# One subtraction of 2048 columns in place of two of 1024, for the low part of a feed-forward's weight block

## The chip, the cores and the metric

The kernel runs on one core of a Trainium2 chip. The metric is device time in microseconds for one execution. The engines are named as the profile names them: PE is TensorE (matmuls; PEld its weight loads), DVE is VectorE, ACT is ScalarE, POOL is GpSimd, SP is SyncE, which issues the transfers.

## The reference

A trunk of two layers on 256 rows of 1024 channels in float32. A layer is half a feed-forward, a mixer, half a feed-forward, each on a normed input and added to the residual; the mixer of layer 0 is a convolution module, that of layer 1 latent attention. The feed-forwards hold most of the work:

```python
D_MODEL = 1024; SEQ = 256; DEPTH = 2; D_FF = 2816
def swiglu_ffn(h, w1, w3, w2):
    return (jax.nn.silu(h @ w1) * (h @ w3)) @ w2

for i in range(DEPTH):
    h = h + 0.5 * swiglu_ffn(rmsnorm(h, ffn_norm1[i]), ffn1_w1[i], ffn1_w3[i], ffn1_w2[i])
    m = rmsnorm(h, mix_norm[i])
    h = h + (conv_module(m, ...) if i % 2 == 0 else mla(m, ...))
    h = h + 0.5 * swiglu_ffn(rmsnorm(h, ffn_norm2[i]), ffn2_w1[i], ffn2_w3[i], ffn2_w2[i])
return rmsnorm(h, final_norm)
```

## The kernel before

**Two parts of every number.** A float32 product is made of three matmuls with fp32r operands (`mm3`, L333 to L337): high by low, high by high, low by high. So each weight block, 128 partitions by 2048 columns, is loaded into a `raw` tile (4 buffers), copied by ACT to `hi` (a rounded copy, a CAST), and DVE subtracts: `lo = raw - hi`. `hi` and `lo` have 5 buffers each. Both are made in two pieces of 1024 columns (`PIECES = 2`), and PE may start on the first piece when its high and low are there. The first matmul that uses a piece takes its low.

**Blocks.** The list `blocks` names all weight blocks in the order of their use. A feed-forward has 39: for the up projection, chunks of 512 hidden columns with four blocks each; for the down projection, blocks of two rows of tiles. An ordinary block is used by 24 matmuls of 512 columns; `load` brings it and splits it (L247, L248).

**Seven products.** One up chunk and the first four blocks of the down projection of each feed-forward are multiplied as a 2x2 block product with seven products in place of eight (`seven`, `load_seven`, `seven_products`). The seven operands are blocks or sums of blocks: DVE makes a sum of 2048 columns in place in a raw tile (`sub` of whole tiles, L201), then the operand is split as any block (L215, L201). The last operand, number 6, is such a sum. Each product is 12 matmuls, so a block lasts PE half as long as an ordinary one. Between products ACT copies a PSUM bank and DVE adds one to another (L259): the add after product 2 and the one after product 4. Two `order` calls tie the first lows of operands 5 and 6 to these adds.

**Around a chunk.** When a chunk's two sums stand in PSUM (`u`), ACT takes the Silu of one (L970) and DVE multiplies (L972, or L259 where the multiplication is marked urgent); that reads the banks, which then serve the next sums (`o` of the down projection among them: PSUM tag A has four). The product `s` is turned (L485, then transfers through DRAM) and split into Gh and Gl (L862): a gate pair.

**Order.** A scheduler places the instructions of each engine from the program's dependencies and its own timeline; `order(a, b)` adds that a comes after b, `behind` puts a cast behind the last urgent instructions of its engine, and `urgent` gives a group priority. Engines run their queues in order.

Of the kernel before, what the change touches and what calls it, by code (L numbers as in the profile page):

```python
# [11 lines left out]
F32 = mybir.dt.float32  # L12
# [7 lines left out]
P = 128  # L20
D = 1024
S = 256
NT = S // P
# [3 lines left out]
HB = 2048  # L27
# [62 lines left out]
def trunk(ctx: ExitStack, tc: tile.TileContext, x, xt, first, pos, invf, gfin, wdw,  # L90
          f1w13, f1w2, f2w13, f2w2, cw1, cw2, wa, wuq, wukv, wo, wpair, out):
    nc = tc.nc
# [12 lines left out]
    def uid(s):  # L105
        n_uid[0] += 1
        return f"{s}_{n_uid[0]}"
# [12 lines left out]
        return [("seven", j, four, group) for j in range(7)]  # L120

    blocks = []
    conv_block = {}
    for i in range(2):
        for w13, w2 in ((f1w13, f1w2), (f2w13, f2w2)):

            n_ffn = 2 * i + (w13 is f2w13)
            for cc_ in range(5):
                if cc_ in SEVEN_UP.get(n_ffn, ()):
                    four = [w13[i, m, 2 * cc_ + a_] for a_ in range(2) for m in range(2)]  # L130
                    blocks += seven(four)
                    continue
                for m in range(2):
                    blocks += [w13[i, m, 2 * cc_ + a_] for a_ in range(2)]
            blocks += [w13[i, a_, 10] for a_ in range(2)]
            if n_ffn in SEVEN_DOWN:
                blocks += seven([w2[i, a_] for a_ in range(4)])
            blocks += [w2[i, a_] for a_ in range(4 if n_ffn in SEVEN_DOWN else 0, NF // 2)]
            if w13 is f1w13:
                if i == 0:  # L140

                    for m in (-1, -2, -3, -4, *CONV_TILES):
                        blocks += [cw2[-m - 1] if m < 0 else ("whole", cw1[m])]
                        conv_block[m] = len(blocks) - 1
                else:
                    blocks += [wa[0], wa[1], wa[2][:, :1280], wa[3][:, :1280]]
                    blocks += [wuq[2], wuq[0], wukv[0], wukv[1], wuq[1]]
                    blocks += [wo[a_] for a_ in range(H // 2)]
    loaded = []
# [8 lines left out]
    def behind(ins):  # L158

        for first in ahead_of.get(ins.ins.engine, [])[-BEHIND:]:  # L160
            order(ins, first)


    casts = {}
# [5 lines left out]
    placed = []  # L170
# [19 lines left out]
    def load_seven(j, four, b, pieces):  # L190
        hi = wp.tile([P, HB], F32R, tag="hi", name=uid("hi"))
        lo = wp.tile([P, HB], F32R, tag="lo", name=uid("lo"))
        n = len(loaded)
        if j == 0:
            b[11], b[12] = fetched(four[0]), fetched(four[1])
        elif j == 1:
            b[22] = fetched(four[3])
        elif j == 2:
            b[21] = fetched(four[2])
        def sub(out, left, right):  # L200
            ins = nc.vector.tensor_sub(out, left, right)  # L201
            behind(ins)
            return ins

        if j == 1:
            sub(b[11], b[12], b[11])
            sub(b[12], b[22], b[12])
        elif j == 2:
            thirds[n] = sub(b[11], b[22], b[11])
        elif j == 6:  # L210
            sub(b[11], b[21], b[11])
        raw = b[(11, 11, 11, 21, 12, 22, 11)[j]]
        for i in range(pieces):
            c = slice(i * HB // pieces, (i + 1) * HB // pieces)
            casts[n, i] = nc.scalar.copy(hi[:, c], raw[:, c]), sub(lo[:, c], raw[:, c], hi[:, c].bitcast(F32))  # L215
            behind(casts[n, i][0])
        return hi, lo

    def load(src, pieces=1):
        if isinstance(src, tuple) and src[0] == "seven":  # L220
            return load_seven(*src[1:], pieces)
        if isinstance(src, tuple):
            raw = rawp.tile([P, HB], F32, tag="raw", name=uid("raw"))
            nc.sync.dma_start(raw, src[1])
            return raw
        n = src.shape[-1]
        there = len(loaded) in raws
        raw = raws.pop(len(loaded))[0] if there else rawp.tile([P, HB], F32, tag="raw", name=uid("raw"))
        hi = wp.tile([P, HB], F32R, tag="hi", name=uid("hi"))
        lo = wp.tile([P, HB], F32R, tag="lo", name=uid("lo"))  # L230
        if there:
            pass
        elif len(loaded) < 7:

            for i in range(pieces if len(loaded) < 4 else 1):
                c = slice(i * n // pieces, (i + 1) * n // pieces) if len(loaded) < 4 else slice(n)
                fetch(raw[:, c], src[:, c])
        else:
            dma = nc.sync.dma_start(raw[:, :n], src)
            if turns:  # L240

                order(dma, turns[-1].ins)
        for i in range(pieces):
            c = slice(i * n // pieces, (i + 1) * n // pieces)

            low = nc.gpsimd if len(loaded) == conv_block[-4] else nc.vector
            casts[len(loaded), i] = (nc.scalar.copy(hi[:, c], raw[:, c]),  # L247
                                     low.tensor_sub(lo[:, c], raw[:, c], hi[:, c].bitcast(F32)))  # L248
            for cast in casts[len(loaded), i] if len(loaded) not in placed else ():
                behind(cast)  # L250
        return hi, lo

# [49 lines left out]
    for k in range(KT):  # L302
        c = slice(k % 4 * 512, k % 4 * 512 + 512)
# [176 lines left out]
    def turn_blocks(pool, src, n, tag, after=(), b=None):  # L480


        w = n * P
        t = pool.tile([P, 512], F32, tag=tag + "t", name=uid(tag + "t"), bufs=2)
        last_turn[0] = nc.vector.transpose(t[:, :w], src.rearrange("p (t j q) -> p j t q", t=n, q=32))  # L485
        d = dram.tile([P, w], F32, tag=tag + "d", name=uid(tag + "d"), bufs=4)
        dv = d.rearrange("(j p) (i c) -> i p j c", p=32, c=32 * n)
        for i in range(4):
            dma = nc.sync.dma_start(dv[i], t[32 * i:32 * i + 32, :w].rearrange("p (j c) -> p j c", j=4))
            for a in after:  # L490
                order(dma, a.ins)
        if b is None:
            b = pool.tile([P, 512], F32, tag=tag + "b", name=uid(tag + "b"), bufs=2)
        last_read[0] = nc.sync.dma_start(b[:, :w], d)
        return b[:, :w].rearrange("p (i t q) -> p t i q", i=4, q=32)

# [346 lines left out]
    gates = []  # L843
# [7 lines left out]
    def ffn_in(act, X, make_next, beside, apart, seven_up, seven_down):  # L851
# [48 lines left out]
        for c in range(6):  # L900
# [18 lines left out]
            for m in range(0 if u else 1 if both else 2):  # L919
                parts = weights(KT // kn, c > 0 or m > 0)  # L920
# [17 lines left out]
                for i, (k, tb, *kinds) in enumerate(steps):  # L938
                    hi, lo = parts[k // kn]
# [35 lines left out]
        if seven_down:  # L975
            both = (xp.tile([P, KT, S], F32R, tag=tag, name=uid("rows")) for tag in ("Xh", "Xl"))
            late = {2: None, 3: None}
            o.seven({**first_form, **forms_of(down_sums[1:], *both, late)}, late)
            for gate in gates[-2 * NT:]:
                for ins, cast in zip(gate, casts[n_used[0] + 1, 0]):  # L980
                    order(ins, cast.ins)
        stage.append("down")
# [456 lines left out]
    def mla_in(act, X, make_next, cc, sn):  # L1439
# [61 lines left out]
        parts = weights(3, False)  # L1501
# [4 lines left out]
        last = None  # L1506
        for tb in range(NT):
# [5 lines left out]
            last = last_low[0]  # L1513
# [37 lines left out]
        for tb in range(NT):  # L1551
            u = bank("A", "qr")
            qu.append(u)
            for k in range(4):
                after = (last,) if k == 0 else turned if (tb, k) == (0, 2) else ()
                last = mm3(u, CQh[:, k, tbs(tb)], CQl[:, k, tbs(tb)], hi[:, k * 512:(k + 1) * 512],
                           lo[:, k * 512:(k + 1) * 512], k == 0, k == 3, after)
# [14 lines left out]
        last = nope(part, QN, 4, CQh, CQl, 512, 0, (0, 4), turned)  # L1572
        for t in range(NT):
            b = transposed(kd[t], 0, 1, (last,))
# [5 lines left out]
        for tb in range(NT):  # L1580
            b = transposed(qr[tb], 0, 4, (last,), turns_of[tb]).rearrange("p (j t) -> p j t", t=P)
            for parity in range(2):
                half, rest = (slice(64 * i, 64 * i + 64) for i in (parity, 1 - parity))
                high = QR[half, parity, :, tbs(tb)]
# [8 lines left out]
        for tb in range(NT):  # L1593
            for d in range(2):
                b = bank("A", "v")
                for k in range(2):
                    c = slice(k * D + d * 512, k * D + d * 512 + 512)
# [7 lines left out]
        score_last, maxima, powers, scaled, copies, late = [], [], [], [], [], []  # L1605

        def scores(hd):
            b = bank("B", "sc")
            sc = {0: b[:, :P], 1: b[:, P:P + S]}
            last = None  # L1610
            for qb in range(NT):
                n = (qb + 1) * P
                three = [(QN[:, hd, tbs(qb)], KN[:, hd, :n]), (QA[hd % 2, qb][:, hd // 2], KA[:, :n]),
                         (QR[:, hd % 2, hd // 2, tbs(qb)], KR[:, hd % 2, :n])]
                for i, (rows_of, keys) in enumerate(three if qb == 0 else three[1:] + three[:1]):
                    mm = nc.tensor.matmul(sc[qb], rows_of, keys, start=i == 0, stop=i == 2)  # L1616
                    if last is not None:
                        order(mm, last.ins)
                    last = mm
            score_last.append(last)  # L1620
            return softmax(sc)
# [52 lines left out]
        for j, i, lows in ((0, 0, maxima[2]), (0, 1, scaled[0]), (1, 0, scaled[1]), (1, 1, scaled[2])):  # L1674
            high, low = casts[n_used[0] + j, i]
# [187 lines left out]
```

## Time and profile before

| | us |
|---|---|
| median of 3 runs | 892.11 |
| lowest, highest | 892.09, 892.71 |
| profiled execution | 891.44 |
| its span in the profile | 889.5 |
| PE busy | 882.0 |
| DVE busy | 770.4 |
| ACT busy | 580.2 |

The span is the time from the first to the last instruction of the profiled execution; the rest of its time lies around it. A row of a timeline gives start and duration in us from the span's start, engine, line, operation, output and input; "x2" is two instructions in a row, and brackets give the idle time before and what ended it.

### The profile page before, as it was taken

What the parts mean: (1) busy time and instruction counts of PE and PEld (TensorE: products, weight loads), DVE (VectorE), ACT (ScalarE), POOL (GpSimd) and SP (SyncE); (2) the same over time, 40 slices, a digit from 0 to 9 for tenths busy, and PEclk for the clock granted to TensorE, in tenths of its full rate; (3) what the DMA queues carried; (4) which work ended last, traced back from release to release, by engine and by line L of the source; (5) the groups of instructions that cost most, each with busy time, mean ns of one, the idle gap of its engine ahead of it and who ended that gap; (6) DMA issues with size and microseconds to landing.
All of it is one profiled execution on the core that took longest, in us unless ns stands there. A gap on an engine that the chain in (4) does not pass through costs nothing.

```text
span 889.5 us, 12294 instructions
## 1 busy us (share of the span) xinstructions
PE 882.0 (99%) x4209; PEld 741.9 (83%) x4209; DVE 770.4 (87%) x1114; ACT 580.2 (65%) x1005; POOL 104.8 (12%) x227
## 2 busy tenths in 40 slices
PE   9999999999999999999999999999999999999997
PEld 7888887898988888888888888888899888888886
DVE  6899999789999998999498989995778689989973
ACT  7667868789887655657275465673676666474752
POOL 1000000079952000000010000001400010000000
PEclk9999999999999999999999999999999999999999
DMA  9884929834216855939759378495643549287541
GB/s 338 297 308 161 398 80 374 300 132 153 96 60 225 307 213 194 365 93 393 251 179 344 97 249 318 142 386 183 221 147 142 190 155 368 80 300 276 192 190 48
DMA packets 71054, 198.94 MB, mean 224 GB/s; under 512 B 12368, under 2 KB 41936, under 8 KB 51664
## 3 DMA queue, kind: packets, MB, share of 16 engines
q1 hardware_dynamic: 70560, 197.47, 61.9%
q8 instruction: 33, 0.54, 0.2%
q10 hardware_dynamic: 432, 0.69, 0.2%
q14 instruction: 29, 0.24, 0.1%
HBM read 181.87 MB, written 16.25 MB: 223 GB/s over the span
## 4 chain that ended last, share of the span: by engine, by line
PE 98%; DVE 1%; issue 0%; ACT 0%; ACTq 0%; DVEq 0%
PE u L333 17%; PE u L337 17%; PE u L336 17%; PE o L333 9%; PE o L337 9%; PE o L336 9%; PE u L1019 3%; PE gate L1019 3%; PE o L1255 3%; PE u L418 2%; PE sc L1616 1%; PE tp L453 1%; PE pairs L1062 1%; DVE lo L201 1%; PE a L337 1%; PE a L336 1%
## 5 line engine op out<-in xcount | busy, mean ns | idle before, releaser
L248 DVE TENSOR_TENSOR lo<-raw,hi 128x1024 fp32r<-128x1024 f32 (+1 forms) x228 | 266.8, 1210 | 29.2 <-ACT hi L247 28.5
L247 ACT CAST hi<-raw 128x1024 fp32r<-128x1024 f32 (+1 forms) x230 | 228.5, 1044 | 72.1 <-DMA raw<-in_f2w 24.3
L337 PE MATMUL u<-hi,Xl 128*128 128x512 f32 x592 | 230.4, 389 | 0.0
L336 PE MATMUL u<-hi,Xh 128*128 128x512 f32 x592 | 230.3, 389 | 0.0
L333 PE MATMUL u<-lo,Xh 128*128 128x512 f32 x592 | 230.2, 389 | 0.0
L215 ACT CAST hi<-raw 128x1024 fp32r<-128x1024 f32 x112 | 111.7, 1049 | 56.7 <-DVE raw L201 46.4
L201 DVE TENSOR_TENSOR lo<-raw,hi 128x1024 fp32r<-128x1024 f32 x112 | 132.0, 1215 | 6.6 <-ACT hi L215 6.5
L337 PEld LDWEIGHTS u<-hi,Xl 128*128 128x128 f32 x592 | 111.1, 188 | 23.6 <-DVE Xl L472 0.5
L336 PEld LDWEIGHTS u<-hi,Xh 128*128 128x128 f32 x592 | 111.1, 188 | 23.1
L333 PEld LDWEIGHTS u<-lo,Xh 128*128 128x128 f32 x592 | 111.1, 188 | 22.9
L333 PE MATMUL o<-lo,Gh 128*128 128x512 f32 (+1 forms) x276 | 106.7, 386 | 0.0
L336 PE MATMUL o<-hi,Gh 128*128 128x512 f32 (+1 forms) x276 | 106.5, 386 | 0.0
L337 PE MATMUL o<-hi,Gl 128*128 128x512 f32 (+1 forms) x276 | 106.5, 386 | 0.0
L444 POOL TENSOR_TENSOR ms<-ss 128x1 f32<-128x1 f32 x16 | 8.1, 509 | 592.8 <-ACT junk L436 592.8
L201 DVE TENSOR_TENSOR raw<-raw,raw 128x2048 f32<-128x2048 f32 x32 | 73.1, 2285 | 0.8 <-DMA raw<-in_f1w 0.2
L333 PEld LDWEIGHTS o<-lo,Gh 128*128 128x128 f32 x276 | 51.8, 188 | 10.6 <-DVE lo L201 0.2
L337 PEld LDWEIGHTS o<-hi,Gl 128*128 128x128 f32 x276 | 51.8, 188 | 10.5
L336 PEld LDWEIGHTS o<-hi,Gh 128*128 128x128 f32 x276 | 51.8, 188 | 10.4
L1108 DVE SCALAR_TENSOR_TENSOR acc<-V,dw,acc 128x128 f32<-128x128 f32 (+1 forms) x174 | 53.9, 390 | 0.0
L970 ACT ACTIVATE s<-u,R 128x512 f32<-128x512 f32 (+1 forms) x48 | 30.9, 647 | 29.5 <-PE u L337 28.7
L1129 ACT ACTIVATE prod<-V,dw 128x128 f32<-128x128 f32 (+1 forms) x128 | 45.6, 415 | 1.9 <-POOL Y L1130 1.0
L806 DVE SCALAR_TENSOR_TENSOR h<-o,rh,h 128x512 f32<-128x512 f32 (+1 forms) x18 | 12.9, 719 | 29.0 <-PE o L337 29.0
(269 smaller groups left out, 1306.6 us busy)
## 6 DMA issues: line engine op xcount, KB each, us to landing
raw<-in_f2w SPq DMA_DIRECT2D x66, 1024.0 KB, 5.6
raw<-in_f1w SPq DMA_DIRECT2D x62, 1024.0 KB, 6.9
raw<-in_cw SPq DMA_DIRECT2D x12, 1024.0 KB, 5.2
gd<-gt SPq DMA_DIRECT2D x160, 64.0 KB, 2.9
gb<-gd SPq DMA_DIRECT2D x24, 256.0 KB, 2.8
rows<-gd SPq DMA_DIRECT2D x16, 256.0 KB, 3.3
raw<-in_wo SPq DMA_DIRECT2D x4, 1024.0 KB, 4.7
hd<-rows SPq DMA_DIRECT2D x56, 64.0 KB, 2.3
```

What stands on the lines that cost most here:

```text
L201: ins = nc.vector.tensor_sub(out, left, right)
L215: casts[n, i] = nc.scalar.copy(hi[:, c], raw[:, c]), sub(lo[:, c], raw[:, c], hi[:, c].bitcast(F32))
L247: casts[len(loaded), i] = (nc.scalar.copy(hi[:, c], raw[:, c]), low.tensor_sub(lo[:, c], raw[:, c], hi[:, c].bitcast(F32)))
L248: low.tensor_sub(lo[:, c], raw[:, c], hi[:, c].bitcast(F32)))
L333: mm = nc.tensor.matmul(o, ah, bl, start=start, stop=False, skip_group_check=seeded)
L336: nc.tensor.matmul(o, ah, bh, start=False, stop=False, skip_group_check=seeded)
L337: return nc.tensor.matmul(o, al, bh, start=False, stop=stop, skip_group_check=seeded)
L970: nc.scalar.activation(s[:, :w], u[0, tb][:, :w], AF.Silu, scale=X.r[tb])
L1019: mm = nc.tensor.matmul(u[:, t], w[:, c], X.x[:, k, t], start=(k == 0), stop=(k == KT - 1))
L1108: dve_last.append(nc.vector.scalar_tensor_tensor(out if j == j1 - 1 else y, v, w, y, op0=ALU.mult, op1=ALU.add))
L1129: prods_last.append(nc.scalar.activation(p, v, AF.Copy, scale=w))
L1255: p = nc.tensor.matmul(o[tb, d], (Zl if kind == "x" else Zh)[:, f, tbs(tb)], (lo if kind == "l" else hi)[:, c], start=(f, kind) == (0, "l" ...
```

## The change

In each feed-forward all blocks but the first four and the last four are entered in `at_once`: 31 of 39, 124 in all. For these the two high casts stay two instructions of 1024 columns, and the low is one subtraction of 2048 columns, which needs both highs. The low then counts as the low of both pieces. Three more edits come with it: `gb` tiles in a feed-forward have three buffers, one more gate pair is ordered behind a cast of the down projection, and the scores of heads 1 and 2 are ordered behind those of the head before.

```diff
+    at_once = set()
...
+            n_first = len(blocks)
...
+            at_once.update(range(n_first + 4, len(blocks) - 4))
...
+        split(n, raw, hi, lo, HB, pieces, nc.vector)
         for i in range(pieces):
-            c = slice(i * HB // pieces, (i + 1) * HB // pieces)
-            casts[n, i] = nc.scalar.copy(hi[:, c], raw[:, c]), sub(lo[:, c], raw[:, c], hi[:, c].bitcast(F32))
-            behind(casts[n, i][0])
+            for cast in casts[n, i] if i == 0 or n not in at_once else casts[n, i][:1]:
+                behind(cast)
         return hi, lo
+
+    def split(n, raw, hi, lo, width, pieces, low):
+        parts = [slice(i * width // pieces, (i + 1) * width // pieces) for i in range(pieces)]
+        if n in at_once:
+            highs = [nc.scalar.copy(hi[:, c], raw[:, c]) for c in parts]
+            whole = low.tensor_sub(lo[:, :width], raw[:, :width], hi[:, :width].bitcast(F32))
+            for i, high in enumerate(highs):
+                casts[n, i] = high, whole
+            return
+        for i, c in enumerate(parts):
+            casts[n, i] = (nc.scalar.copy(hi[:, c], raw[:, c]),
+                           low.tensor_sub(lo[:, c], raw[:, c], hi[:, c].bitcast(F32)))
...
-            b = pool.tile([P, 512], F32, tag=tag + "b", name=uid(tag + "b"), bufs=2)
+            b = pool.tile([P, 512], F32, tag=tag + "b", name=uid(tag + "b"), bufs=3 if tag == "g" else 2)
...
-            for gate in gates[-2 * NT:]:
+            for gate in gates[-2 * NT - 1:]:
                 for ins, cast in zip(gate, casts[n_used[0] + 1, 0]):
                     order(ins, cast.ins)
...
-            last = None
+            last = score_last[-1] if 0 < hd < 3 else None
```

The scheduler places the instructions anew. In the rows below, names carry their tile numbers, which differ between the two programs, and the lines of the program after are its own: the split is L226 (high) and L227 (low), sums of blocks L205, adds L271, Silu L982, multiplication L984.

DVE at the end of the up group of seven in the second feed-forward, before: the lows of operands 3, 4 and 5, the add after product 2, the sum for operand 6, the add after product 4, the low of operand 6.

```order
L201 TENSOR_TENSOR lo_3481<-raw_3304,hi_3480 128x1024 x2
L201 TENSOR_TENSOR lo_3501<-raw_3362,hi_3500 128x1024
L259 TENSOR_TENSOR u_3460<-u_3458,p_561_3498 128x512
L201 TENSOR_TENSOR lo_3501<-raw_3362,hi_3500 128x1024
L201 TENSOR_TENSOR raw_3302<-raw_3372,raw_3302 128x2048
L259 TENSOR_TENSOR u_3459<-u_3458,p_561_3498 128x512
L201 TENSOR_TENSOR lo_3520<-raw_3302,hi_3519 128x1024 x2
```

The same place after:

```order
L227 TENSOR_TENSOR lo_3438<-raw_3265,hi_3437 128x2048
L271 TENSOR_TENSOR u_3418<-u_3416,p_561_3454 128x512
L227 TENSOR_TENSOR lo_3457<-raw_3322,hi_3456 128x2048
L205 TENSOR_TENSOR raw_3263<-raw_3331,raw_3263 128x2048
L271 TENSOR_TENSOR u_3417<-u_3416,p_561_3454 128x512
L227 TENSOR_TENSOR lo_3475<-raw_3263,hi_3474 128x2048
```

The first half of operand 5's low stood ahead of the add; the whole low now stands behind it, and the sum for operand 6 behind both.

ACT at the start of the down projection of the same feed-forward, before: high casts, the Silu of the last chunk's two parts (256 columns), more high casts.

```order
L215 CAST hi_3797<-raw_3703 128x1024 x2
L862 CAST Gh_2920<-gb_3623 128x4x128
L970 ACTIVATE s_3866<-u_3816,R_2859 128x256
L215 CAST hi_3807<-raw_3703 128x1024 x2
L215 CAST hi_3906<-raw_3809 128x1024 x2
L366 CAST rows_3898<-rows_139 128x512
L970 ACTIVATE s_3880<-u_3817,R_3006 128x256
```

The same place after:

```order
L226 CAST hi_3744<-raw_3651 128x1024 x2
L226 CAST hi_3753<-raw_3651 128x1024 x2
L226 CAST hi_3851<-raw_3755 128x1024 x2
L982 ACTIVATE s_3811<-u_3761,R_2828 128x256
L378 CAST rows_3843<-rows_139 128x512
L982 ACTIVATE s_3825<-u_3762,R_2975 128x256
```

The first Silu moved behind four high casts, and the gate's high cast (Gh) to a later place.

DVE there, before: a sum of blocks, the multiplication of the last chunk's first part, its turn, two lows.

```order
L862 TENSOR_TENSOR Gl_2921<-gb_3623,Gh_2920 128x4x128
L485 STREAM_TRANSPOSE gt_3778<-s_3775 128x512
L201 TENSOR_TENSOR raw_3703<-raw_3799,raw_3703 128x2048
L972 TENSOR_TENSOR s_3866<-s_3866,u_3816 128x256
L485 STREAM_TRANSPOSE gt_3869<-s_3866 128x256
L201 TENSOR_TENSOR lo_3808<-raw_3703,hi_3807 128x1024 x2
L201 TENSOR_TENSOR lo_3907<-raw_3809,hi_3906 128x1024 x2
```

The same place after:

```order
L497 STREAM_TRANSPOSE gt_3725<-s_3722 128x512
L205 TENSOR_TENSOR raw_3651<-raw_3746,raw_3651 128x2048
L227 TENSOR_TENSOR lo_3754<-raw_3651,hi_3753 128x2048
L227 TENSOR_TENSOR lo_3852<-raw_3755,hi_3851 128x2048
L984 TENSOR_TENSOR s_3811<-s_3811,u_3761 128x256
```

The multiplication moved behind two lows, the turn of its result with it, and the gate's low out of this place.

More of the change, by code (lines that the diff above doesn't have):

```diff
@@ L242, in load @@
                 order(dma, turns[-1].ins)
[L243 to L249, printed above, removed]
+        split(len(loaded), raw, hi, lo, n, pieces, nc.gpsimd if len(loaded) == conv_block[-4] else nc.vector)
+        for i in range(pieces if len(loaded) not in placed else 0):
+            for cast in casts[len(loaded), i] if i == 0 or len(loaded) not in at_once else casts[len(loaded), i][:1]:
                 behind(cast)
```

## The prediction

> **What bounds the kernel now.** First the page: the span and the shares of the engines.
>
> ```profile
> span 889.5 us, 12294 instructions
> PE 882.0 (99%) x4209; PEld 741.9 (83%) x4209; DVE 770.4 (87%) x1114; ACT 580.2 (65%) x1005; POOL 104.8 (12%) x227
> ```
>
> TensorE (PE) is busy for all but 7.5 us. VectorE (DVE), where the change takes work away, is at 87%, and its time counts only where PE waits for it. The waits of PE, named by line, and the chain that ended last show that such places are few now:
>
> ```profile
> PE o L333 <- DVE lo L201: 0.4, 1, 0.4
> ...
> 1.04 3.99 PE warm L325 x21
> 5.03 22.22 PE u L418 x96
> ...
> 136.75 0.47 PE o L333
> ```
>
> So a faster DVE can give back about half a microsecond, and any new PE wait is added to the span in full: nothing gives PE time back. The question is when each low part is ready, against when PE wants it. The groups by form give the sizes:
>
> ```profile
> L248 DVE TENSOR_TENSOR lo<-raw,hi 128x1024 fp32r<-128x1024 f32 x224 | 263.8, 1217 | 29.2 <-ACT hi L247 28.5
> L201 DVE TENSOR_TENSOR lo<-raw,hi 128x1024 fp32r<-128x1024 f32 x112 | 132.0, 1215 | 6.6 <-ACT hi L215 6.5
> L201 DVE TENSOR_TENSOR raw<-raw,raw 128x2048 f32<-128x2048 f32 x32 | 73.1, 2285 | 0.8 <-DMA raw<-in_f1w 0.2
> ```
>
> A half costs 1.22 us, and a whole I take from the third row: 2.29 us (same operation and width, f32 written instead of fp32r).
>
> **The tight place: the end of a group of seven products.** In the timeline of the second feed-forward's up group, DVE, then ScalarE (ACT), then PE:
>
> ```profile
> 345.57 1.22 DVE L201 TENSOR_TENSOR lo<-raw,hi 128x1024 fp32r<-128x1024 f32 x1 [1.25 <-ACT hi L215]
> 346.71 0.69 DVE L259 TENSOR_TENSOR u<-u,p 128x512 f32<-128x512 f32 x1
> 347.31 1.22 DVE L201 TENSOR_TENSOR lo<-raw,hi 128x1024 fp32r<-128x1024 f32 x1
> 348.44 2.29 DVE L201 TENSOR_TENSOR raw<-raw,raw 128x2048 f32<-128x2048 f32 x1
> 351.21 0.70 DVE L259 TENSOR_TENSOR u<-u,p 128x512 f32<-128x512 f32 x1 [0.49 <-PE u L337]
> 351.84 2.36 DVE L201 TENSOR_TENSOR lo<-raw,hi 128x1024 fp32r<-128x1024 f32 x2
> ...
> 350.76 2.01 ACT L215 CAST hi<-raw 128x1024 fp32r<-128x1024 f32 x2 [1.58 <-DVE raw L201]
> ...
> 345.57 0.39 PE L333 MATMUL u<-lo,Xh 128*128 128x512 f32 x1
> 351.01 0.39 PE L333 MATMUL u<-lo,Gh 128*128 128x512 f32 x1
> 353.73 0.39 PE L333 MATMUL u<-lo,Xh 128*128 128x512 f32 x1
> ```
>
> Products are counted from 0. PE begins product 3 at 345.57, 5 at 351.01, 6 at 353.73: 2.72 us each. The last block is a sum that DVE makes (348.44), whose highs ACT then makes (350.76), and of whose low DVE makes the first half at 351.84, as soon as the first high is there (0.03 us after 350.76 + 1.05). That half ends at 353.06 and PE starts on it at 353.73. A stalled start in the first down group shows what lies between a half's end and PE:
>
> ```profile
> 133.18 2.28 DVE L201 TENSOR_TENSOR raw<-raw,raw 128x2048 f32<-128x2048 f32 x1
> 135.38 2.35 DVE L201 TENSOR_TENSOR lo<-raw,hi 128x1024 fp32r<-128x1024 f32 x2
> ...
> 136.75 0.47 PE L333 MATMUL o<-lo,rows 128*128 128x512 f32 x1 [0.40 <-DVE lo L201]
> 137.05 0.40 PE L336 MATMUL o<-hi,rows 128*128 128x512 f32 x1
> ```
>
> The first half ends at 136.60; the next matmul comes at 137.05 where 0.23 after 136.82 would be full pace: 0.2 us. So the margin in the up group is 353.73 - 353.06 - 0.2 = 0.47 us.
>
> **The change, part by part.**
>
> *DVE time.* 124 pairs become wholes. A pair takes 2.35 (row 135.38), a whole 2.29: 0.06 each, 7.4 us in all. None of it is on PE's path, except at 136.75. [...]
>
> *Term A: the last product of a group.* In the changed order the add that follows product 2 stands ahead of the low of block 5, so the chain begins when PE ends product 2, wherever DVE stands: add 0.20 us after product 3's first matmul (351.21 against 351.01); add to next 0.60 (346.71 to 347.31); whole low to next 2.20 (a 2048 row, 133.18 to 135.38); sum to first high 2.32 (348.44 to 350.76); both highs 2.01; 0.03; whole low 2.29; to PE 0.2. That is 9.85 us, and PE has three products, 8.16. PE waits 1.7 us. The two causes: 1.0 us for the second high, 1.1 us for the second half. What DVE saved earlier cannot help, because the chain starts from PE's own end. It holds for seven of the eight groups (four up, three down): 11.9 us, bounds 10.5 and 12.6 (1.5 and 1.8 each: nothing between low and PE, or 0.3).
>
> *Term A', the first down group.* There the sum stands ahead of block 5's low, and PE waits already (136.75). A whole ends 1.07 us later than the half, bound from below 1.1; the add in front waits for more work than before, up to 1.3 more. I take 1.7.
>
> After each group DVE has a multiplication (0.60) and a whole (2.20) for 2.72 us of PE: 0.08 more, five times, 0.4 us.
>
> *Term B: the first whole of the program.*
>
> ```profile
> 24.44 2.00 ACT L247 CAST hi<-raw 128x1024 fp32r<-128x1024 f32 x2 [0.36 <-DMA raw<-in_f1w]
> ...
> 25.52 1.23 DVE L248 TENSOR_TENSOR lo<-raw,hi 128x1024 fp32r<-128x1024 f32 x1 [5.09 <-ACT hi L247]
> ...
> 27.09 0.39 PE L333 MATMUL u<-lo,Xh 128*128 128x512 f32 x1
> ```
>
> Highs end at 26.44; + 0.03 + 2.29 + 0.2 = 28.96 against 27.09: 1.9 us. A multiplication (0.60) stands ahead of it now, under the highs; bounds 1.5 (the block lands earlier by the 0.36 that ACT waited for it) and 2.2 (half of the 0.60 comes late).
>
> *Term C: a PSUM bank given back later.* In the second to fourth feed-forwards' down groups, product 1 writes a bank that a 256-column multiplication (L972) must have read. In the changed order four high casts stand ahead of its Silu on ACT, and two whole lows ahead of it on DVE; the casts wait for a DVE sum.
>
> ```profile
> 384.54 2.25 DVE L201 TENSOR_TENSOR raw<-raw,raw 128x2048 f32<-128x2048 f32 x1
> 387.08 0.42 DVE L972 TENSOR_TENSOR s<-s,u 128x256 f32<-128x256 f32 x1 [0.29 <-ACT s L970]
> ...
> 388.02 4.63 DVE L201 TENSOR_TENSOR lo<-raw,hi 128x1024 fp32r<-128x1024 f32 x4
> ...
> 391.81 0.39 PE L333 MATMUL o<-lo,s1h 128*128 128x512 f32 x1
> ...
> 559.36 2.25 DVE L201 TENSOR_TENSOR raw<-raw,raw 128x2048 f32<-128x2048 f32 x1
> ...
> 565.89 0.39 PE L333 MATMUL o<-lo,s1h 128*128 128x512 f32 x1
> ...
> 821.26 2.25 DVE L201 TENSOR_TENSOR raw<-raw,raw 128x2048 f32<-128x2048 f32 x1
> ...
> 828.79 0.39 PE L333 MATMUL o<-lo,s1h 128*128 128x512 f32 x1
> ```
>
> Before, the multiplication ends at 387.50, 4 us ahead of PE. After: the sum ends at 386.79, less 0.60 (a 512-column operation, as 346.71 to 347.31) because a gate's low (L862) moved behind it; + 0.03 + 2.01 highs + 0.03 + 2 x 2.20 + 0.42 + 0.2 = 393.28 against 391.81: 1.5 us. The same from 561.61: 2.2, and from 823.51: 1.2. Together 4.9; bounds 0, where DVE comes earlier by 2 us, and 6.7, where the 0.60 isn't saved.
>
> *Cheap edits.* The third buffer of gb costs space and hides the later gate lows. The extra gate pair that is held back is the 0.60 above. The order of three heads' score matmuls moves work of one size inside PE's queue, without a wait that the order shows: 0, bounds -0.3 and 0.3. A raw buffer is freed when its second half has been read, as before, so the weight loads do not move by more than the low does. Behind a waiting low stand multiplications, transposes and with them SP's turn DMAs; where they reach PE is terms A and C.
>
> **Sum.** 11.9 + 1.7 + 0.4 + 1.9 + 4.9 = 20.8 us. The profiled execution took 891.44 us (span 889.5 and 1.9 around it), which becomes 912.2; the median of the runs is 0.67 us above the profiled one: 913.
>
> **Rivals.**
> - *Forecast*: 913, its own range 908 to 918: 0.72.
> - *The banks are free in time*: term C falls away, 908. For it: the wholes take 0.06 us less each, and DVE idles 36 us before its lows (29.2 + 6.6 in the groups). Against: eight wholes stand between two groups, 0.5 us, and three times 1.2 to 2.2 is wanted. 0.10.
> - *TensorE's clock drops after each wait.* At the start 21 matmuls of 256 columns took 3.99 us (0.19 each) where later 96 of 512 took 22.22 (0.23): 0.74 ns a column against 0.45. If each of 12 waits over 1 us brought 3 us at that pace, 3 x (1 - 0.45/0.74) = 1.2 us each, 14 us: 927. Against: the wait at 136.75 was followed by full pace. [...] 0.08.
> - *Not slower.* The mechanism: the chain does not start from PE's end but from DVE's queue, and DVE, 0.06 us earlier per block, has the last block's sum made before PE ends product 2. It decides at the first add: if the sum of term A ends 2.2 us (1.7 and the 0.47 margin) earlier than I place it, PE waits nowhere, and the waits at 136.75 go too: 891.4 - 0.4, 891 to 892 as measured. Against: the order puts the sum behind the add and the whole low. 0.06.
> - *More than one of these together, or a wait I did not see*: 0.04.
>
> **The numbers.** A measurement of this kernel can tell 0.2% (1.8 us) from no change. The range 905 to 920 holds the forecast and the free banks: the lower bounds of A, A' and B without C are 10.5 + 1.1 + 1.5 = 13.1 (891.44 + 13.1 + 0.67 = 905), the upper ones with C and 0.08 after all eight groups 12.6 + 2.4 + 2.2 + 6.7 + 0.6 = 24.5 (917), and 3 us are for a wait I did not see; it leaves out the clock and the case without loss. Slower 0.94; same 0.04 and faster 0.02 out of "not slower".
>
> **What would show it.** In the profile after: PE waits for DVE lo (the split's line) about ten times, 1.7 us each at the last product of a group, the highs' second half ending 0.03 us before the whole low begins; three waits of 1 to 2 us for the multiplication L972 at the first s1h product; DVE busy about 18 us less by single durations (124 x (2 x 1.217 - 2.29)); PE's clock unchanged. Wrong would be: waits of PE under 0.5 us, a whole low that starts before its second high, or the sum ahead of the add in the up groups.

## The result

The kernel after took 915.55 us (median of six runs, 913.75 to 918.41) against 892.24 us before (891.94 to 893.05): a ratio of 1.0262, 95% interval 1.0246 to 1.0278. The change makes the kernel 23.3 us slower, where 20.8 were forecast, and the time lies in the forecast's range of 905 to 920. The profiled execution took 915.71 us. First the head of its page and, from the view of waits, what PE waited for (us in total, times, the longest):

```profile
span 913.9 us, 12149 instructions
PE 886.9 (97%) x4209; PEld 740.8 (81%) x4209; DVE 761.8 (83%) x990; ACT 579.2 (63%) x1005; POOL 105.8 (12%) x227
...
PE u L345 <- DVE lo L227: 8.0, 5, 2.1
PE o L345 <- DVE lo L227: 6.0, 4, 1.5
PE o L345 <- DVE s L984: 4.6, 3, 2.1
...
PE o L345 <- DVE o L271: 0.7, 1, 0.7
PE u L430 <- ACT Xh L659: 0.5, 2, 0.4
PE u L345 <- ACT Xh L617: 0.2, 1, 0.2
```

DVE is busy for less time and PE waits. Lines after the split are 12 further down than before: L227 is the low of a whole, L233 that of a half, L205 a sum of blocks, L271 the add of two banks, L984 the last multiplication of a gate. Nine waits are for a whole low (term B, the seven groups of term A, and one of A'), three for L984 (term C), and one for L271 (the other part of A'). The mean granted clock was 0.999.

The end of the second feed-forward's up group after, the place the prediction worked through, DVE, then ACT, then PE:

```profile
352.81 0.70 DVE L271 TENSOR_TENSOR u<-u,p 128x512 f32<-128x512 f32 x1 [0.65 <-PE u L349]
353.42 2.28 DVE L227 TENSOR_TENSOR lo<-raw,hi 128x2048 fp32r<-128x2048 f32 x1
355.62 2.28 DVE L205 TENSOR_TENSOR raw<-raw,raw 128x2048 f32<-128x2048 f32 x1
...
359.97 2.29 DVE L227 TENSOR_TENSOR lo<-raw,hi 128x2048 fp32r<-128x2048 f32 x1 [1.09 <-ACT hi L226]
...
357.94 2.00 ACT L226 CAST hi<-raw 128x1024 fp32r<-128x1024 f32 x2 [1.78 <-DVE raw L205]
...
357.99 0.39 PE L345 MATMUL u<-lo,Gh 128*128 128x512 f32 x1
362.32 0.50 PE L345 MATMUL u<-lo,Xh 128*128 128x512 f32 x1 [1.46 <-DVE lo L227]
```

The add begins as PE ends product 2 (0.65 us of waiting on PE). Behind it stand the whole low of operand 5 and the sum. The highs follow at 357.94, the whole low at 359.97, 0.03 us after the second high, and PE begins product 6 at 362.32, 4.33 us after product 5, where before it was 2.72: 1.6 us late. The step from the matmul that waited to the next one is 0.34 us in place of 0.23, so 0.11 more is lost at each place of terms A, B and C. At the two places of A' that step was as long before the change, and nothing is added.

The start of that feed-forward's down projection, in the same order of engines:

```profile
392.80 2.25 DVE L205 TENSOR_TENSOR raw<-raw,raw 128x2048 f32<-128x2048 f32 x1
397.19 4.49 DVE L227 TENSOR_TENSOR lo<-raw,hi 128x2048 fp32r<-128x2048 f32 x2 [2.14 <-ACT hi L226]
401.60 0.41 DVE L984 TENSOR_TENSOR s<-s,u 128x256 f32<-128x256 f32 x1
...
398.96 0.46 ACT L982 ACTIVATE s<-u,R 128x256 f32<-128x256 f32 x1
...
402.07 0.50 PE L345 MATMUL o<-lo,s1h 128*128 128x512 f32 x1 [1.30 <-DVE s L984]
```

The Silu ran at 398.96, long before DVE came to its multiplication (401.60); that stood behind two wholes (4.41 us), and these behind the highs of a sum.

One thing in the order listings above needs a correction in words. The half of operand 5's low that stood ahead of the add before the change was its second half: it waits for ACT there (1.25 us at 345.57 in the prediction's rows), and the half behind the add waits for nothing. The line `order(casts[n0 + 5, 0][1], add.ins)` binds the low that `casts` keeps for the first half, so that half stands behind the add. With a whole low, both entries of `casts` are the same instruction, so an order written for one half now holds up the entire block.

### The profile page after: what moved, and what is told of

Its sections match the earlier page's. It is cut to its first block, busy times and chain, and to the rows that moved or that the text cites. A ratio compares the mean times of both kernels' runs of the same rounds, so it can differ in the third digit from the quotient of the medians.

```text
span 913.9 us, 12149 instructions
## 1 busy us (share of the span) xinstructions
PE 886.9 (97%) x4209; PEld 740.8 (81%) x4209; DVE 761.8 (83%) x990; ACT 579.2 (63%) x1005; POOL 105.8 (12%) x227
## 4 chain that ended last, share of the span: by engine, by line
PE 66%; DVE 16%; DMA 8%; issue 6%; ACT 3%; SPq 1%; DVEq 0%; ACTq 0%
PE u L345 9%; PE u L349 8%; PE u L348 8%; PE o L345 8%; DVE lo L227 8%; PE o L348 7%; PE o L349 7%; DVE raw L205 3%; PE u L1031 3%; PE gate L1031 3%; ACT hi L226 2%; DMA raw<-in_f1w 2%; PE u L430 2%; DMA raw<-in_f2w 2%; DMA gd<-gt 1%
## 5 line engine op out<-in xcount | busy, mean ns | idle before, releaser
L226 ACT CAST hi<-raw 128x1024 fp32r<-128x1024 f32 x248 | 245.8, 1048 | 128.2 <-DVE raw L205 82.0
L227 DVE TENSOR_TENSOR lo<-raw,hi 128x2048 fp32r<-128x2048 f32 x124 | 281.8, 2282 | 42.2 <-ACT hi L226 42.1
L233 DVE TENSOR_TENSOR lo<-raw,hi 128x1024 fp32r<-128x1024 f32 (+1 forms) x92 | 106.8, 1203 | 14.6 <-ACT hi L232 14.2
L232 ACT CAST hi<-raw 128x1024 fp32r<-128x1024 f32 (+1 forms) x94 | 92.9, 1035 | 28.3 <-PE o L349 13.8
L456 POOL TENSOR_TENSOR ms<-ss 128x1 f32<-128x1 f32 x16 | 10.1, 634 | 610.5 <-ACT junk L448 610.5
L205 DVE TENSOR_TENSOR raw<-raw,raw 128x2048 f32<-128x2048 f32 x32 | 73.1, 2285 | 0.5
L982 ACT ACTIVATE s<-u,R 128x512 f32<-128x512 f32 (+1 forms) x48 | 30.9, 647 | 23.8 <-PE u L349 23.0
```

Source lines behind the costliest of these rows:

```text
L226: highs = [nc.scalar.copy(hi[:, c], raw[:, c]) for c in parts]
L227: whole = low.tensor_sub(lo[:, :width], raw[:, :width], hi[:, :width].bitcast(F32))
L232: casts[n, i] = (nc.scalar.copy(hi[:, c], raw[:, c]), low.tensor_sub(lo[:, c], raw[:, c], hi[:, c].bitcast(F32)))
L982: nc.scalar.activation(s[:, :w], u[0, tb][:, :w], AF.Silu, scale=X.r[tb])
```

## Experiments

Ten kernels, in three groups, each timed beside the kernel before. Ratios are to it; the medians of before lay between 891.99 and 892.49 us.

| kernel | us | ratio, 95% interval |
|---|---|---|
| side edits alone | 892.00 | 0.9991 (0.9981 to 1.0000) |
| after, gates held back as before | 906.44 | 1.0144 (1.0121 to 1.0167) |
| after, last operands in halves | 905.01 | 1.0127 (1.0102 to 1.0151) |
| wholes for the last operands alone | 900.99 | 1.0083 (1.0060 to 1.0105) |
| wholes in blocks 5 to 11 alone | 892.25 | 1.0002 (0.9992 to 1.0011) |
| after, operand 5's low free of the add | 913.52 | 1.0227 (1.0186 to 1.0268) |
| after, halves near the groups' ends | 895.94 | 1.0044 (1.0027 to 1.0062) |
| halves, but the second high made first | 898.79 | 1.0072 (1.0057 to 1.0087) |
| after, the sum ahead of operand 5's low | 903.13 | 1.0126 (1.0109 to 1.0143) |
| the same, gates held back as before | 909.16 | 1.0179 (1.0150 to 1.0209) |

**Is the saved DVE time worth anything?** Wholes only where blocks are made well ahead:

```diff
-            at_once.update(range(n_first + 4, len(blocks) - 4))
+            at_once.update(n for n in range(n_first + 4, len(blocks) - 4) if 5 <= n - n_first < 12)
```

> The kernel after with wholes only in the seven blocks 5 to 11 of each feed-forward, well ahead of its groups of seven (28 of 124), all others in halves. Theory: DVE's saved time is off the path, so it is worth nothing, and a whole costs nothing where its block is made well ahead of PE: 892.2, same as before within 0.5. Rival: the saved DVE time counts, 28 x 0.06 to 0.16 = 1.7 to 4.5 us less: 888 to 890.5. Other rival: any whole delays PE by its second half: 900 or more.

Measured 892.25, no difference: 28 wholes neither help nor hurt. Its waits of PE are those of before (the start, and 0.4 us in the first down group). A shorter DVE brings nothing because PE waits for it in that one place, and a whole costs nothing where there is slack. The loss of the full change is therefore a matter of place.

**The last operand of a group alone.**

```diff
-            at_once.update(range(n_first + 4, len(blocks) - 4))
+            at_once.update(n for n in range(n_first + 4, len(blocks) - 4) if isinstance(blocks[n], tuple) and blocks[n][1] == 6)
```

> The kernel after with wholes only for the last operand of the eight groups (8 of 124), all others in halves, side edits as in the kernel after. If the second half alone were the price, with the margin of 0.47 us that the profile of before showed: 0.6 x 7 + 1.1 = 5.3, 897.5. If the low also waits for the second high, which a first half didn't, the chain is 1.07 + 0.9 to 1.0 longer less the 0.47: 1.2 to 1.6 in the up groups, 0.7 in the down groups, 1.1 in the first down group, counted through the order about 9: 901. Rival: the loss comes from the amount of wholes and not from these eight: 892 to 893.

Measured 900.99: eight wholes out of 124 cost 8.5 us, more than a third of the whole loss. In the second feed-forward's up group, DVE and PE:

```profile
354.21 0.70 DVE L271 TENSOR_TENSOR u<-u,p 128x512 f32<-128x512 f32 x1 [0.49 <-PE u L349]
355.78 2.29 DVE L227 TENSOR_TENSOR lo<-raw,hi 128x2048 fp32r<-128x2048 f32 x1 [0.87 <-ACT hi L226]
...
358.13 0.50 PE L345 MATMUL u<-lo,Xh 128*128 128x512 f32 x1 [1.24 <-DVE lo L227]
```

The sum and the add stand as before the change (the sum ends 0.49 us before the add begins). DVE has room, and waits 0.87 us for the second high before the low begins. PE's step into product 6 is 1.40 us longer, and 0.11 is lost at the matmul behind: 1.5. The prediction's two causes and the margin give 1.0 + 1.07 - 0.47 = 1.6. In the down groups it is 0.6 to 0.7, in the first of them 1.0.

**The second high by itself.** All lows in halves; for the last operand the second half's high is made first, so the first half's low has to wait for both:

```diff
-            at_once.update(range(n_first + 4, len(blocks) - 4))
+            at_once.update(n for n in range(n_first + 4, len(blocks) - 4) if False)
...
+        if isinstance(blocks[n], tuple) and blocks[n][0] == "seven" and blocks[n][1] == 6:
+            highs = [nc.scalar.copy(hi[:, c], raw[:, c]) for c in parts[::-1]][::-1]
+            for i, c in enumerate(parts):
+                casts[n, i] = highs[i], low.tensor_sub(lo[:, c], raw[:, c], hi[:, c].bitcast(F32))
+            return
```

> The kernel after with every low in halves, side edits kept; for the last operand of each group alone ACT makes the second half's high first, so that the first low must wait for both highs, as a whole would, but stays 1024 columns. It prices the second high by itself. If both causes count as in the prediction (1.0 for the second high, 1.1 for the second half, less the margin of 0.47): about 0.6 at the last product in place of the 1.2 to 1.6 of wholes, and the second low is ready when PE wants it: 0.5 to 0.7 x 7 + 1.0 = 4.5 to 6, 896.5 to 898. Counted through the order, where the low and the sum ahead of it shift too, up to 7: 899. Rival: a second high costs nothing, since DVE comes late anyway: 892.

Measured 898.79, at the upper count. Its ACT and PE rows at the same group (lines 5 further down):

```profile
353.08 1.05 ACT L232 CAST hi<-raw 128x1024 fp32r<-128x1024 f32 x1 [1.58 <-DVE raw L205]
354.03 0.61 ACT L879 CAST Gh<-gb 128x512 fp32r<-128x512 f32 x1
354.55 1.05 ACT L232 CAST hi<-raw 128x1024 fp32r<-128x1024 f32 x1
...
356.91 0.50 PE L350 MATMUL u<-lo,Xh 128*128 128x512 f32 x1 [0.70 <-DVE lo L234]
```

A gate's cast slipped in between the two highs, so this kernel makes the first low wait for 1.47 us more (353.08 to 354.55), not 1.0. Less the margin of 0.47 that is 1.0; the step measures 0.86 + 0.11. So waiting for the second high costs in full, also when the low stays 1024 columns wide. The second half has no run of its own: the run with the last operand alone loses 1.5 us, of which the second high gives 1.0 less the 0.47, and the rest is left for the half.

**What the sum's place is worth.** After, with one order more:

```diff
         elif j == 6:
-            sub(b[11], b[21], b[11])
+            order(casts[n - 1, 0][1], sub(b[11], b[21], b[11]).ins)
```

> The kernel after, with one more order: the whole low of operand 5 waits for the sum that makes operand 6, so the sum stands in front of it on DVE and not behind. Theory: term A's chain holds the whole low's 2.20 us ahead of the sum. Without it, from PE's end of product 2: 0.20 + 0.60 + 2.20 (sum) + 2.20 (low of operand 5) + 0.60 (second add) + 2.29 (low of operand 6) + 0.2, with some idle time = 8.4 to 8.7 against PE's 8.16: 0.3 to 0.6 at the last product in place of 1.7, 0.1 at the one before, and the wholes after the group are no longer late: 9 to 10.5 less than after, 905 to 907. Rival: only the second half and the second high of the last operand count, wherever its sum stands: 914 to 916.

Measured 903.13, 12.4 less than after, more than expected. DVE and PE at the same group:

```profile
350.65 2.28 DVE L205 TENSOR_TENSOR raw<-raw,raw 128x2048 f32<-128x2048 f32 x1
352.85 2.28 DVE L227 TENSOR_TENSOR lo<-raw,hi 128x2048 fp32r<-128x2048 f32 x1
...
356.01 4.48 DVE L227 TENSOR_TENSOR lo<-raw,hi 128x2048 fp32r<-128x2048 f32 x2
...
358.35 0.50 PE L345 MATMUL u<-lo,Xh 128*128 128x512 f32 x1 [0.16 <-DVE lo L227]
```

The sum and the two wholes are the same instructions as after; only the sum has changed place with a whole low. PE waits 0.16 in place of 1.46. So in the kernel after the 2.2 us of that low in front of the sum are needed for the full loss, beside the second half and the second high. In the run with the last operand alone half of that low (350.31 to 351.44) stands between the add and the sum, as before the change, and 1.5 us are lost. The order moved elsewhere too: of term C two waits are left, 2.5 us in all in place of 4.6, which is the part that the expectation did not have. The last feed-forward now pays 1.3 at the block behind its up group, and 0.11 at the matmul behind.

**Whether the add's order anchors the chain.** The line quoted in the result is taken out of the kernel after:

```diff
-        order(casts[n0 + 5, 0][1], add.ins)
```

> The kernel after without the order that puts operand 5's low behind the add that follows product 2; nothing else changes. The whole low then stands ahead of the add. If that order is the cause of term A (the chain anchored at PE's end of product 2), the waits at the last product go: 915.6 - 11 = 904 to 905. Rival: DVE's queue is as long either way, so the last sum and low come only 0.6 to 0.7 earlier, while the add, 2 us later, gives its PSUM bank to product 4 late by 0.4 to 0.5 (1.1 in the third up group): 914 to 915.

Measured 913.52, but its four runs spread from 910.11 to 917.34 and the interval takes in the kernel after: in the total this is undecided. Two executions took 910.1 and 910.6 us, two 916.5 and 917.3, and what separates them is not known. The trace is of one of the slower two (916.49). In its view of waits of PE:

```profile
PE u L345 <- DVE lo L227: 4.7, 5, 1.5
PE o L345 <- DVE lo L227: 3.9, 4, 1.5
...
PE o L345 <- DVE o L271: 1.1, 4, 0.7
...
PE u L345 <- DVE u L271: 1.0, 1, 1.0
```

The waits for whole lows fall from 14.0 to 8.6 us and do not go, and new ones come for the add (L271), now late with its bank. Steps into product 6 are 0.93 to 1.03 longer than before in place of 1.6 to 2.3. So the order of low and add is a part of the cause and not the whole of it.

**Is the lateness handed on?** The last operand of each group in halves, all else as after:

```diff
-            at_once.update(range(n_first + 4, len(blocks) - 4))
+            at_once.update(n for n in range(n_first + 4, len(blocks) - 4) if not (isinstance(blocks[n], tuple) and blocks[n][1] == 6))
```

> The kernel after, with the low of the last operand of all eight groups in halves again (116 wholes left). Simple reading of term A: the eight waits at the last product go and nothing else changes: 915.6 - 14 = 901 to 902. Rival: in the up groups DVE's lateness is only handed on, since the block behind the group is a whole as well and its low waits for the same queue: four waits of about 1.7 stand there instead, while the down groups' waits go; counted through the changed order with the profile's durations 904 (902.5 to 906).

Measured 905.01, as the rival has it. DVE and PE behind the second up group:

```profile
356.92 2.36 DVE L233 TENSOR_TENSOR lo<-raw,hi 128x1024 fp32r<-128x1024 f32 x2
...
360.55 2.25 DVE L227 TENSOR_TENSOR lo<-raw,hi 128x2048 fp32r<-128x2048 f32 x1
...
362.85 0.50 PE L345 MATMUL u<-lo,Xh 128*128 128x512 f32 x1 [1.37 <-DVE lo L227]
```

Product 6 is in time, and the next block's whole low, behind the halves, a multiplication and a transpose (0.6 each), makes PE wait 1.37 us one product later. The wait is not bound to one block: whichever whole comes first where DVE has no slack pays. The waits of the three later down groups went: there the next whole comes right behind the halves, without a multiplication and a transpose between (at 413.62 in the second feed-forward, and PE takes it at 416.17 without a wait). The first down group still waits (1.15 us), at operand 5.

**All tight places in halves.**

```diff
-            at_once.update(range(n_first + 4, len(blocks) - 4))
+            at_once.update(n for n in range(n_first + 4, len(blocks) - 4) if n > 4 and n - n_first not in (17,18,19,20,21,30,31,32,33,34))
```

> The kernel after with halves at the first block of the program (block 4), at the last two operands of each group and the three blocks behind it; all other 83 or so wholes stay, side edits too. Theory: the loss sits at these places; the third to fifth operands of a group and the first blocks of the down groups still cost a little, counted through the order about 3 us: 893.5 to 896, with no wait over 0.8 us. Rival: the loss is handed on to whichever whole comes next, as in the run with the last operands alone in halves: 900 to 905.

Measured 895.94, 4 us above before and 19.6 below after. The view of groups lists 83 wholes and 170 halves, so 41 wholes are gone. In its profiled execution (898.66, the longest of four) no wait for a low is over 0.5 us. DVE at the second feed-forward's down start:

```profile
390.48 0.41 DVE L984 TENSOR_TENSOR s<-s,u 128x256 f32<-128x256 f32 x1
...
392.68 4.49 DVE L227 TENSOR_TENSOR lo<-raw,hi 128x2048 fp32r<-128x2048 f32 x2 [1.31 <-ACT hi L226]
```

The two wholes that stood ahead of the multiplication are still wholes, but now stand behind it, and PE does not wait for L984. So term C's 5.4 us went with an order that was chosen anew, and not because these blocks are in halves. What the 41 wholes cost by themselves is the rest of the 19.6, some 14 us, if the two can be told apart at all; the 83 that stay, in this order and with the side edits, cost 4.

**The side edits.** The kernel before with the three of them:

```diff
-            b = pool.tile([P, 512], F32, tag=tag + "b", name=uid(tag + "b"), bufs=2)
+            b = pool.tile([P, 512], F32, tag=tag + "b", name=uid(tag + "b"), bufs=3 if tag == "g" else 2)
...
-            for gate in gates[-2 * NT:]:
+            for gate in gates[-2 * NT - 1:]:
...
-            last = None
+            last = score_last[-1] if 0 < hd < 3 else None
```

> The kernel before with the three side edits alone (a third gate buffer, one more gate pair held back, the order of three heads' scores), every low in halves. The prediction's step: they cost nothing, 892.2 us with 0.5 either way, no new wait of TensorE. Rival: the side edits carry a part of the loss themselves; if the held-back gate pair alone puts the 256-column multiplications late, three waits of 1 to 2 us, about 897.

Measured 892.00, and PE's waits are those of before: alone they cost nothing. But the kernel after without the second of them:

```diff
-            for gate in gates[-2 * NT - 1:]:
+            for gate in gates[-2 * NT:]:
```

> The kernel after, with the held-back gates as before (two pairs of heads, not one more); all 124 wholes stay. The prediction's step: the pair that moved away saves DVE 0.60 us ahead of each of the three late multiplications, so without the edit each of these waits grows by 0.6: 915.6 + 1.8 = 917.4. Rival: the edit is what lets the high casts and whole lows overtake the last chunk's Silu and multiplication; the order without it has them ahead of the casts, so the three waits (4.6 us listed, 5 with what the next matmul loses) go, and the wholes behind them start early enough that the ends of the down groups wait less too: 907 to 910.

Measured 906.44: 9 us less than after, and not 1.8 more. DVE, then ACT, at the second feed-forward's down start, and from the view of waits what PE waits for:

```profile
396.53 0.41 DVE L984 TENSOR_TENSOR s<-s,u 128x256 f32<-128x256 f32 x1
398.73 4.49 DVE L227 TENSOR_TENSOR lo<-raw,hi 128x2048 fp32r<-128x2048 f32 x2 [1.31 <-ACT hi L226]
...
394.45 0.48 ACT L982 ACTIVATE s<-u,R 128x256 f32<-128x256 f32 x1 [3.91 <-DVE gt L497]
...
PE u L345 <- DVE lo L227: 7.3, 5, 1.5
PE o L345 <- DVE lo L227: 4.2, 4, 1.4
```

Here the Silu stands ahead of the casts and the multiplication ahead of the two wholes, as before the change: the order was chosen anew, and term C is gone. By the PE steps that is 5.4 us of the difference; most of the rest lies in shorter waits of the later down groups and of the third up group. To see whether the held-back pair or that order does it, the same edit was undone in the kernel with the sum first, where the casts and wholes keep their place ahead of the multiplication:

> As the run with the sum in front of operand 5's low, with the held-back gates as in the kernel before. Here the order has the four high casts and two whole lows ahead of the last chunk's Silu and multiplication although the gate edit is gone. If the held-back pair itself delays the banks: another 9 less, 896 to 897. If it is the casts and lows ahead of the multiplication: the three waits for L984 are there, each 0.6 longer than with the pair held back, as the prediction priced it: 1.8 more than the other run, 907 to 909.

Measured 909.16 against 903.13 for the one with the edit (four executions from 903.81 to 910.15, so even the shortest is far from 896 to 897). The three waits for L984 are there (4.9 us, the longest 2.6), so it is the place of the multiplication that counts. That each grows by 0.6 is not shown: by the PE steps of the two traces they change by -0.8, from nothing to 2.2, and by +1.2, since the order differs in more than the pair. Nor are these waits the larger part of the 6 us: the spans of the two traces differ by 5.3 us, and some 3.2 of them are the clock, told at the end.

## Why the prediction was right, and what was mis-sized

PE issues 4209 matmuls before and after, so each term can be read as how much later a matmul begins in the one trace than in the other.

- *What bounds the kernel.* PE was 99% busy and all that came new was paid in full: the time from PE's first matmul to its last grew by 24.4 us, and so did the span. The parts below come to some 24.0; the rest is scattered over small steps.
- *DVE time.* By the groups' busy time the lows take 10.2 us less (266.8 + 132.0 before, 281.8 + 106.8 after, rows below); I had 7.4 from the pair. None of it reached PE, as the run with wholes in blocks 5 to 11 shows. Added up by single durations, which count an overlap of neighbours twice (the pair at 135.38 took 2.35, two single halves 2.43), they take 18.3 less, where the prediction had 18. The measured busy time lies between 7.4 and 18, nearer to the pair. The 0.16 us a block in the rival of the run with wholes in blocks 5 to 11 is shown by no run: by single durations it is 0.15 (2 x 1.217 - 2.282), by busy time 0.08 (10.2 / 124).

```profile
L248 DVE TENSOR_TENSOR lo<-raw,hi 128x1024 fp32r<-128x1024 f32 (+1 forms) x228 | 266.8, 1210 | 29.2 <-ACT hi L247 28.5
...
L227 DVE TENSOR_TENSOR lo<-raw,hi 128x2048 fp32r<-128x2048 f32 x124 | 281.8, 2282 | 42.2 <-ACT hi L226 42.1
L233 DVE TENSOR_TENSOR lo<-raw,hi 128x1024 fp32r<-128x1024 f32 (+1 forms) x92 | 106.8, 1203 | 14.6 <-ACT hi L232 14.2
```

- *Term A*, 11.9 forecast: 12.9. Six of the seven places measure 1.7 to 1.8, as worked out. The third feed-forward's up group measures 2.4: there the add did not follow PE at once, since DVE was still at a whole low when product 2 ended. So "wherever DVE stands" failed at this one place, by 0.6 us. Of the two causes named, the second high is shown by the run that makes it first, and the second half by what the run with the last operand alone loses beyond that. The chain as such is shown by the run with the sum first. That DVE's earlier finish could not help is right for the same reason: it waits for PE's product 2 in six of the seven.
- *Behind the groups*, 0.4 forecast: 0.5, of which 0.3 behind the late group.
- *Term A'*, 1.7 forecast: 1.8, in two parts, as the next rows of the kernel after show (DVE, then PE): the add gives a bank late (0.7), and then the whole low is late (1.06, where 1.07 was worked out). The add's share had only a bound, up to 1.3, so that 1.7 came so near is in part luck.

```profile
140.64 2.28 DVE L227 TENSOR_TENSOR lo<-raw,hi 128x2048 fp32r<-128x2048 f32 x1
...
138.58 0.50 PE L345 MATMUL o<-lo,rows 128*128 128x512 f32 x1 [0.70 <-DVE o L271]
143.07 0.47 PE L345 MATMUL o<-lo,rows 128*128 128x512 f32 x1 [1.45 <-DVE lo L227]
```

- *Term B*, 1.9 forecast: 1.7.
- *Term C*, 4.9 forecast: 5.4 (1.6, 2.3, 1.5). The step by step working holds to 0.1 us in the second and third feed-forwards, and to 0.3 in the fourth. What failed is its attribution: I put the held-back gate pair among the cheap edits and credited it with 0.60 at each place. The runs show that the side edits cost nothing without the wholes and the wholes 9 us less without that edit, because it decides which order comes out.
- *Outside the forecast*, 1.5 us: 0.9 in the first microseconds of the program and 0.6 at the start of the second feed-forward, with waits for Xh at both places (in the list of waits). Traces of other kernels have such a wait or have none (1.5 us once in the run without the add's order, none with wholes in blocks 5 to 11), so I take it for a scatter of single executions; that was not tested.

So the mechanism held, and the 20.8 us fell short of what came by a little in each of terms A and C and by the 1.5 us that were not forecast. Of the rivals, free banks and no loss are refuted by the rows. The clock's drop did not come in the profiled execution of the kernel after, but see below; no run shows the 3 us at the slow pace that its rival was worked out from, and the slow stretch told at the end lasted about 3.4.

## What to carry to other kernels

An instruction that does two pieces of work at once is also ready for neither until it has both inputs (the whole low at 359.97 began 0.03 us after the second high), and everything that was written against the first piece (here an order) now waits for the second. Before merging, find where the consumer takes the first piece as soon as it is there: here halves at 41 of 124 places took back some four fifths of the loss, a part of it through an order that was chosen anew, and 28 wholes elsewhere cost nothing and brought nothing. Cost small order edits together with the change that they come with; alone they may measure zero, and together 9 us.

## What the hardware showed that was not expected

In the run with the sum first and the gates as before, PE's clock was halved (0.50 from 577 to 579) soon after two of its waits. The view of windows (PEclk in the column behind POOL) around the first, and PE's rows there:

```profile
575.00:577.00 2.00, 2.00 (x7) 1.64 (x8) 2.00 (x5) 1.54 (x2) 0.00 (x0) 0.73 0.00 0
577.00:579.00 2.00, 2.00 (x6) 1.52 (x6) 2.00 (x3) 0.00 (x0) 0.00 (x0) 0.50 0.25 51
...
574.87 0.50 PE L345 MATMUL o<-lo,s1h 128*128 128x512 f32 x1 [2.01 <-DVE s L984]
...
575.90 0.61 PE L348 MATMUL o<-hi,s1h 128*128 128x512 f32 x1
576.30 0.63 PE L349 MATMUL o<-hi,s1l 128*128 128x512 f32 x1
...
578.86 0.61 PE L349 MATMUL o<-hi,s1l 128*128 128x512 f32 x1
```

One microsecond after the wait's end, eight matmuls follow each other at 0.43 us in place of 0.23: about 3.4 us at half pace, 1.6 us lost, where the prediction's rival had 1.2. The same came 1.5 us after the end of a wait of 2.55 us in the last feed-forward. In the kernel after, a wait of 2.12 us was followed by full pace (three matmuls in 0.69 us):

```profile
542.34 0.50 PE L345 MATMUL u<-lo,Xh 128*128 128x512 f32 x1 [2.12 <-DVE lo L227]
...
543.14 0.39 PE L345 MATMUL u<-lo,Xh 128*128 128x512 f32 x1
543.83 0.39 PE L345 MATMUL u<-lo,Xh 128*128 128x512 f32 x1
```

Waits of 2.0 us or more came in other traces too: 2.12 and 2.07 in the kernel after, and up to 2.2 in the run without the add's order. Only the two here were followed by a drop, and no trace shows one after a shorter wait: the mean granted clock was 0.994 in this profiled execution and 0.998 or 0.999 in all others. So a drop can follow a wait of 2.0 us and need not follow one of 2.2. What decides is not shown. So the drop that the prediction made a rival with 0.08 does happen in one of these kernels. The other five executions of the kernel after have a mean clock of 0.996 to 0.998 and no trace, so drops in them are not excluded; the shortest of all, 913.75, is among those with 0.996.
